# One store of a DMA-bound batched matmul split over two queues, eight engines for a quarter of it

## Chip, cores, metric

The kernel runs on one core of a Trainium2 chip. The metric is the device time of one execution in microseconds (us). All runs quoted here were in the fast state: the granted clock was 0.937 of full speed in the profile before.

## The reference

```python
# x: (32, 512, 1024) float32, weight: (32, 1024, 768) float32
def reference(x, weight):
    return np.matmul(x, weight).astype(np.float32)
```

## The kernel before

For each of 32 batches the kernel loads x (2 MB of float32 in DRAM) and weight (3 MB), converts both to bf16 on the way in (the page counts 1,024 KB for a load of x), transposes x on TensorE, multiplies, and stores 1.5 MB of float32. Every transfer but one is issued from GpSimd to one software queue: in each pass x of batch b+3, then the weights of batch b+3, then the store of batch b−1. Only the store of the last batch goes on SP's queue, in two halves.

```python
AHEAD = 3
...  # cut: pools (w and x 4 buffers, out 7), CHUNKED: weights of the last 4 batches in pieces
out_view = out.rearrange("b (mi mo) n -> b mi (mo n)", mi=P)     # 128 rows of 12,288 B a batch

def load_x(b):
    xs[b] = x_pool.tile([P, MT, K], BF16, name="x_sb")
    nc.gpsimd.dma_start(out=xs[b], in_=x_view[b])
...  # cut: load_w (alike), transpose, matmuls, evacuate

for b in range(B):
    if b + AHEAD < B:
        load_x(b + AHEAD)
        load_w(b + AHEAD)
    if b > 0:
        nc.gpsimd.dma_start(out=out_view[b - 1], in_=outs[b - 1])
    outs[b] = out_pool.tile([P, MT * N], F32, name="out_sb")
    ...  # cut: transposes, matmuls and evacuations of batch b
    # last batch only, after each half:
    #     nc.sync.dma_start(out_view[b, :, cols], outs[b][:, cols])
```

## Time and profile before

| | before |
|---|---|
| time, median of 3 runs | 518.48 us (517.94 to 518.51) |
| software DMA queue, share of 16 engines | 99.9% |
| PE busy | 424.2 us, 82% |
| PE idle for weights | 61.9 us |
| x of the last batch, first and last of 16 landings | 484.26 and 488.88 us |

These are lines of the page of the kernel before: span, busy times, DMA queues (packets, MB, share of 16 engines' span), the summary of the chain that ended last, and the stores as DMA issues (count, KB each, median us from issue to landing).

```profile
span 516.5 us, 5888 instructions
PE 424.2 (82%) x2512; PEld 277.7 (54%) x2560; DVE 127.0 (25%) x192; ACT 76.3 (15%) x129; POOL 53.9 (10%) x106
...
q0 software_dynamic: 14400, 132.65, 99.9%
q1 hardware_dynamic: 288, 1.57, 0.7%
q8 instruction: 20, 0.33, 0.2%
...
DMA 74%; PE 21%; DVE 2%; issue 1%; ACT 0%; POOL 0%; POOLq 0%
...
out_dram<-out_sb POOLq DMA_DIRECT2D x31, 1536.0 KB, 41.9
...
out_dram<-out_sb SPq DMA_DIRECT2D x2, 768.0 KB, 7.0
```

The DMA engines have no idle time: the software queue alone takes 99.9% of them. The 20 packets of q8, which the profile calls an instruction queue, are of 16,384 B and 0.885 to 0.975 us each in the trace; what they carry it does not say. They share engines with the data: each of them sets one engine's data back by about 1.1 us.

The end of the chain of waits (start, duration, what) shows what the last part of the run hangs on.

```profile
457.72 31.16 DMA x_sb<-in_x_dram
488.88 0.04 issue
488.92 0.75 PE pt L67 x4
489.67 1.30 PE pm L85 x8
...
495.00 6.83 PE pm L85 x42
501.88 4.84 PE pm L85 x29
506.74 0.59 ACT out_sb L98
```

PE waits until x of the last batch has landed, at 488.88 us, and has work from there to the end of its own part, near 506.7 us; the last transfer to land is the last store, at 514.61 us. The landing of x is complete only when the last of the 16 engines has delivered its share. Each transfer counts up 16 times, once per engine (the trace has 1,600 packets of 4 B in the software queue for its 100 transfers), so the trace gives the 16 landing times of each. In the kernel before their spread grows from 0.75 us in the first 30 us to 4.62 us for this x. The engines run ahead of or behind each other inside the queue, and PE is fed at the pace of the last.

### The profile page before, as it was taken

How to read it: one execution, taken by the hardware profiler on the slowest of the kernel's cores; microseconds unless marked ns; L12 is line 12 of the kernel's file. 1: busy time of each engine (PE TensorE's matmuls, PEld its weight loads, DVE VectorE, ACT ScalarE, POOL GpSimd, SP SyncE). 2: the span in 40 equal slices, each digit the busy share in tenths (PEclk: the TensorE clock that was granted, in tenths of full speed). 3: DMA queues.
4: the chain of work that ended last, by engine and by line, in shares of the span. 5: the costliest groups of instructions: out<-in, count | busy, mean ns of one | idle time of the engine just before them, and what ended most of it. 6: DMA issues, size and time to landing. Idle time of an engine off the chain costs nothing.

```text
span 516.5 us, 5888 instructions
## 1 busy us (share of the span) xinstructions
PE 424.2 (82%) x2512; PEld 277.7 (54%) x2560; DVE 127.0 (25%) x192; ACT 76.3 (15%) x129; POOL 53.9 (10%) x106
## 2 busy tenths in 40 slices
PE   1799999788887979868897879887887986978992
PEld 1466666455554656545564546554555653655561
DVE  1133333133131331322321213312223121322221
ACT  0011111111111111101110101111111110111111
POOL 3011010100101001100011010010100101111000
PEclk9999999899897998989998979998899897988997
DMA  8999999999999999999999999999999999999996
GB/s 158 217 218 216 211 274 278 272 268 240 263 274 275 278 249 246 279 275 274 266 233 270 278 275 271 245 256 278 273 276 255 245 273 272 276 266 242 256 387 265
DMA packets 14714, 134.60 MB, mean 261 GB/s; under 512 B 1632, under 2 KB 1632, under 8 KB 3040
## 3 DMA queue, kind: packets, MB, share of 16 engines
q0 software_dynamic: 14400, 132.65, 99.9%
q1 hardware_dynamic: 288, 1.57, 0.7%
q8 instruction: 20, 0.33, 0.2%
q14 instruction: 6, 0.05, 0.0%
HBM read 167.77 MB, written 50.33 MB: 422 GB/s over the span
## 4 chain that ended last, share of the span: by engine, by line
DMA 74%; PE 21%; DVE 2%; issue 1%; ACT 0%; POOL 0%; POOLq 0%
DMA w_sb<-in_weight_dram 37%; DMA out_dram<-out_sb 24%; PE pm L85 19%; DMA x_sb<-in_x_dram 13%; PE pt L67 2%; DVE xT L69 1%; DVE out_sb L97 1%; ACT out_sb L98 0%; POOL x_sb L53 0%; POOLq L53 0%; POOLq L59 0%; POOLq L159 0%
## 5 line engine op out<-in xcount | busy, mean ns | idle before, releaser
L85 PE MATMUL pm<-w_sb,xT 128*128 128x256 bf16 (+1 forms) x2000 | 370.7, 340 | 66.6 <-DMA w_sb<-in_weight_dram 61.9
L85 PEld LDWEIGHTS <-xT 128*128 128x128 bf16 x2048 | 207.2, 102 | 204.6 <-issue 72.9
L69 DVE COPY xT<-pt 128x1024 bf16<-128x1024 bf16 x128 | 85.8, 689 | 264.0 <-PE pt L67 264.0
L67 PE MATMUL pt<-ident,x_sb 128*128 128x128 f32 x512 | 80.3, 291 | 15.9 <-DMA x_sb<-in_x_dram 15.6
L67 PEld LDWEIGHTS pt<-ident,x_sb 128*128 128x128 f32 x512 | 76.3, 207 | 24.1 <-issue 14.6
L96 ACT COPY out_sb<-pm 128x512 f32<-128x512 f32 x64 | 37.5, 586 | 287.9 <-PE pm L85 284.5
L97 DVE COPY out_sb<-pm 128x512 f32<-128x512 f32 x64 | 43.9, 687 | 116.2 <-PE pm L85 116.2
L98 ACT COPY out_sb<-pm 128x512 f32<-128x512 f32 x64 | 37.5, 586 | 142.4 <-PE pm L85 142.2
L53 POOL DMA_DIRECT2D x_sb<-in_x_dram x32 | 17.1, 536 | 192.6 <-DMA w_sb<-in_weight_dram 141.8
L59 POOL DMA_DIRECT2D w_sb<-in_weight_dram x37 | 19.7, 532 | 114.2 <-DMA out_dram<-out_sb 56.5
L115 POOL DMA_DIRECT2D out_dram<-out_sb x31 | 16.6, 536 | 136.8 <-DMA x_sb<-in_x_dram 64.7
L96 ACT ACT_TABLE_LOAD x1 | 1.3, 1283 | 0.7 <-PEq L159 0.7
masks.py:199 POOL TENSOR_SCALAR_AFFINE_SELECT ident<-ident 128x128 f32<-128x128 f32 x1 | 0.3, 288 | 0.1
masks.py:197 POOL MEMSET ident<- 128x128 f32 x1 | 0.2, 243 | 0.0
L159 POOL MEMSET const-float32-0.0<- 128x1 f32 x1 | 0.1, 99 | 0.2 <-issue 0.2
L159 POOL MEMSET const-bfloat16-1.0<- 128x1 bf16 x1 | 0.1, 103 | 0.0
L159 POOL MEMSET const-uint8-127<- 128x1 uint8 x1 | 0.1, 103 | 0.0
L159 POOL MEMSET const-float32-1.0<- 128x1 f32 x1 | 0.1, 100 | 0.0
## 6 DMA issues: line engine op xcount, KB each, us to landing
out_dram<-out_sb POOLq DMA_DIRECT2D x31, 1536.0 KB, 41.9
w_sb<-in_weight_dram POOLq DMA_DIRECT2D x28, 1536.0 KB, 43.2
x_sb<-in_x_dram POOLq DMA_DIRECT2D x32, 1024.0 KB, 39.6
w_sb<-in_weight_dram POOLq DMA_DIRECT2D x7, 768.0 KB, 31.4
out_dram<-out_sb SPq DMA_DIRECT2D x2, 768.0 KB, 7.0
w_sb<-in_weight_dram POOLq DMA_DIRECT2D x2, 384.0 KB, 28.7
```

The lines of the kernel that those rows point to most:

```text
L53: nc.gpsimd.dma_start(out=xs[b], in_=x_view[b])
L59: nc.gpsimd.dma_start(out=ws[b][:, at:at + n, :], in_=w_view[b, :, at:at + n, :])
L67: nc.tensor.transpose(pt[:, j, :], pairs[:, mt, j::JT], ident)
L69: nc.vector.tensor_copy(xT.rearrange("p j m r -> p (j m r)"), pt.bitcast(BF16).rearrange("p j m -> p (j m)"))
L85: nc.tensor.matmul(pm[bank][:, at:at + size], xT[:, ko // 2, :, ko % 2], ws[b][:, ko, off:off + size], start=(ko == 0 and not (together an ...
L96: nc.scalar.copy(o[:, 0:512], pm[0])
L97: nc.vector.tensor_copy(o[:, 512:1024], pm[1])
L98: nc.scalar.copy(o[:, 1024:N2], pm[2])
L115: nc.gpsimd.dma_start(out=out_view[b - 1], in_=outs[b - 1])
L159: nc = _bacc.Bacc("TRN2", target_bir_lowering=False, num_devices=1)
```

## The change

The intent is to balance the engines. If some engines are late because they also carry packets of the instruction queue, giving them fewer bytes of one store would let all of them end together. The store of batch 8 is cut: 32 of its 128 rows go as four transfers of eight rows on SP's queue, the other 96 as before.

```diff
+    FEW = {8}
 ...
+    def store(b):
+        first = 0
+        if b in FEW:
+            first = 32
+            for at in range(4):
+                nc.sync.dma_start(out_view[b, at:first:4], outs[b][at:first:4])
+        nc.gpsimd.dma_start(out=out_view[b, first:], in_=outs[b][first:])
 ...
             if b > 0:
-                nc.gpsimd.dma_start(out=out_view[b - 1], in_=outs[b - 1])
+                store(b - 1)
```

The order of instructions on PE, DVE, ACT and GpSimd is unchanged; SP gets four issues.

## The prediction

The sum came to 518.48 - 0.9 = 517.6 us. Terms of it are cut below, because they rested on a rule about the numbers of the engines that no trace here shows: two rows of 0.46 us more, 0.92 us, on each of the eight engines that the 8-row transfers use, and two rows less on each of the other eight. "0-7" and "8-15", here and in the expectations, stand for these two halves and say nothing of the engines' numbers.

> What bounds the kernel. The 16 DMA engines. The page's queue table has the software queue at 99.9% of 16 engines' span, and the chain of waits is 74% DMA, 21% PE. PE is 82% busy and waits 61.9 us for weights. Slack lies only between the engines. The trace's landing records (16 increments per transfer, one per engine) show it: first to last increment is 0.75 us in the first 30 us, 2.4 us at 150 us, 3.5 us at 250 us, 4.6 us from 420 us on. Single engines fall back in steps of about 1.1 us, at the times of the 20 packets of 16,384 B on the instruction queue (about 0.94 us each). The steps go round eight engines in turn (the one hit at 222 us is hit again at 421 us), so about eight engines are never hit, and the four hit at 421 to 496 us end 3.9 to 4.6 us late.[...] The last store lands at 511.1 us on the first engine, at 514.6 us on the last.
>
> What the change does. For batch 8 only, 32 of 128 rows of 12,288 B go as four 8-row transfers.[...] The other 96 rows are 6 per engine.[...] A store row took 0.46 us in the trace[...]. Bytes and the work of PE, DVE, ACT and its order stay; four issues on SP, idle until 506 us, are added.
>
> Critical path. The slowest engine sets the landings of weights and x, and those set PE: x of the last batch lands at 488.9 us, then PE is busy to 506.7 us. If the late engines lie in 8-15, everything after batch 8's store leaves the queue moves 0.9 us earlier; the early engines have about 2 us of slack from 150 us on and do not become the latest. If the late four lie in 0-7, the end is 0.9 us later. This trace gives no engine numbers. That eight engines are hit, and that the amount moved (1.84 us between the halves) fits the spread at that time (2.4 us), makes me believe that the change aims at the right half: three in four.
>
> Prediction: 518.48 - 0.9 = 517.6 us, range 516.7 to 519.4. Chances: faster by over 2% 0.005; within 2% 0.99; slower 0.005.
>
> What would show it. The landing spread after about 190 us falls by about 0.9 us (3.5 to 2.6, 4.6 to 3.7); the hardware queue has about 1.97 MB; x of the last batch lands near 488.0 us; PE busy stays 424 us; the SP stores of batch 8 land within a few us, not 42.
>
> What would make it wrong. The late engines are in 0-7 (then 519.4).[...] PE near its own limit could hide the gain, but it waits on DMA until 489 us.

## The result

The median of six runs is 519.49 us (518.84 to 520.16), against 518.13 us (517.75 to 518.51) for six runs of the kernel before. The ratio of fast runs is 1.0028, 95% interval 1.0015 to 1.0041. A ratio here is the mean time of one kernel's fast runs over that of the other's of the same rounds, so it is not quite the ratio of the medians quoted. The change costs about 1.4 us; the sign is clear, and it is not the predicted one.

The same lines of the page of the changed kernel:

```profile
span 518.1 us, 5899 instructions
PE 425.9 (82%) x2512; PEld 278.1 (54%) x2560; DVE 127.0 (25%) x192; ACT 76.3 (15%) x129; POOL 53.9 (10%) x106
...
q0 software_dynamic: 14368, 132.26, 99.5%
q1 hardware_dynamic: 352, 1.97, 0.9%
q8 instruction: 20, 0.33, 0.2%
...
DMA 88%; PE 9%; issue 1%; DVE 0%; ACT 0%; POOL 0%; POOLq 0%
...
out_dram<-out_sb POOLq DMA_DIRECT2D x30, 1536.0 KB, 42.0
...
out_dram<-out_sb SPq DMA_DIRECT2D x2, 768.0 KB, 5.3
out_dram<-out_sb POOLq DMA_DIRECT2D x1, 1152.0 KB, 41.0
...
out_dram<-out_sb SPq DMA_DIRECT2D x4, 96.0 KB
```

The 0.4 MB moved from q0 to q1 as planned, and nothing else in the totals changed. The chain's share of DMA, 74% before and 88% after, is not evidence of anything: DMA and PE are both mostly busy (99.9% and 82% before), and the chain follows whichever ended last at each step. The control below, which is the kernel before in another spelling, shows 82%.

The end of the chain of the changed kernel:

```profile
459.99 31.17 DMA x_sb<-in_x_dram
491.16 0.04 issue
491.20 0.75 PE pt L68 x4
491.95 1.85 PE pm L86 x8
...
498.92 6.83 PE pm L86 x42
505.80 4.83 PE pm L86 x29
510.65 0.59 ACT out_sb L99
```

The last x landed at 491.16 us, 2.28 us later than before, where the prediction had it near 488.0. From there to the start of the last copy PE took 19.5 us, against 17.9 us before. The windows view (window, its length, busy us and count by engine, clock, DMA share, GB/s) of the last stretch, kernel before and then the changed one:

```profile
488.00:512.00 24.00, 17.68 (x110) 11.38 (x112) 5.47 (x8) 4.64 (x8) 0.53 (x1) 0.94 0.98 365
```

```profile
488.00:512.00 24.00, 19.31 (x110) 12.23 (x112) 5.47 (x8) 4.65 (x8) 0.53 (x1) 0.93 0.92 331
```

The same 110 matmuls took 1.63 us more. In the changed kernel a stretch of 3.4 us at half the clock began at 492.6 us; before, none lay between 478.4 and 509.2 us. This is put down to chance and not to the change: the control below had such a stretch at 488.9 us and still took 517.81 us, and a repeat of the changed kernel had none in this place and took 520.5 us. Nor did it add to the loss: the last store landed at 516.87 us against 514.61 us before, 2.26 us later, which is the delay of the last x and no more.

The landing records are the better witness, because they show all 16 engines. The mean over the 16 landings says how much work the engines had on average; the last says when PE can go on. "Control" is the kernel before rebuilt in the new spelling, with no batch split. Worked out from the landing records, in us, mean and last:

```
transfer           before            control           changed           changed minus control
x of batch 13      200.85 / 202.19   200.77 / 202.35   200.84 / 203.41   +0.07 / +1.06
weights of 13      208.15 / 209.46   208.06 / 209.57   208.71 / 211.75   +0.65 / +2.18
store of 15        306.95 / 309.02   306.96 / 309.22   307.55 / 311.29   +0.59 / +2.07
store of 20        386.15 / 388.02   386.17 / 388.22   386.75 / 390.27   +0.58 / +2.05
x of batch 31      486.25 / 488.88   486.27 / 489.08   486.85 / 491.16   +0.58 / +2.08
```

The x of batch 13 is the first transfer after the split store. By its end the mean is back where it was (+0.07), as it must be if only rows were exchanged, and the last engine is 1.06 us late; at the store of batch 4, before SP's rows, it had been 0.13 us late. Then, within one weight load, the mean itself moves by 0.58 us and the last engine by 1.12 us more, and neither comes back. The second step was not in the prediction at all: no rows were moved there.

Its source can be seen in the packets. A weight row of one engine takes 0.926 us as a packet. Between 203 and 212 us the control has no weight packet over 0.96 us; the changed kernel has 16, the longest 2.29, 2.15 and 1.96 us. Added up, packets in 204 to 212 us are 7.5 us too long. 7.5 us over 16 engines is 0.47 us, most of the 0.58 us. No other cause was found in the trace: PE, DVE, ACT and GpSimd execute the same order, and GpSimd's nearest issue (204.02 to 204.56 us) ends before the first long packet (205.12 us).

The first step is the one that the prediction described, on the wrong engines. The packet records name no engine, but an engine's packets follow each other with fixed gaps (the 0.460 us store rows of one engine start 0.456 to 0.457 us apart at 144.55 to 146.84 us), and the four transfers on SP mark eight of them, so that single engines can be followed through the trace. Lag behind the most advanced engine, in us, of five engines of the changed kernel ("low": carries SP's rows, "high": does not; "q8": start of its 16,384 B packets):

```
engine        at 143 us  at 175 us  at 199 us  at 207 us  at 484 us   q8 at us
low,  late      2.71       4.43       4.11       4.76       6.74      53, 247, 448
low,  late      1.30       3.03       2.70       2.88       4.87      33, 223, 423
high, late      2.01       1.87       2.01       3.10       5.34      74, 273, 475
high, late      1.95       1.81       2.05       3.26       4.18      103, 299
high, first     0.14       0.00       0.01       0.00       0.00      none
```

SP's rows put 1.73 us on both low engines; the 96-row store, with six rows for every engine instead of eight, does not take that back relative to the high ones. So the step is 1.84 us between the halves, as costed (four rows of 0.46 us). But two of the late engines were low ones, and they were the two that had been hit first. After that the two high ones lose 1.1 to 1.2 us between 199 and 207 us, in the long packets.

SP's transfers themselves behaved as predicted. In the timeline of the changed kernel (start, duration, what) SP issues them in three microseconds:

```profile
144.64 3.02 SPq L107 DMA_DIRECT2D out_dram<-out_sb  x4
```

Their landings are at 145 to 156 us. Each has nine increments, one at once (145.81 us for the first) and eight later (150.23 to 151.10 us), and eight packets of 4 B, so eight engines moved data; which eight by number the trace does not show. In the packets SP's rows alternate with packets of the software queue one by one: on one engine an SP row of 0.473 us starts at 148.98 us, then come an x row of 0.624 us, SP's 4 B packet, another x row, and at 150.66 us SP's next row.

### The profile page after: what moved, and what is told of

Same layout as the page of the kernel before. It is cut to its first block, busy times and chain, and to the rows that moved or that the text cites. A ratio compares the mean times of both kernels' runs of the same rounds, so it can differ in the third digit from the quotient of the medians.

```text
span 518.1 us, 5899 instructions
## 1 busy us (share of the span) xinstructions
PE 425.9 (82%) x2512; PEld 278.1 (54%) x2560; DVE 127.0 (25%) x192; ACT 76.3 (15%) x129; POOL 53.9 (10%) x106
## 3 DMA queue, kind: packets, MB, share of 16 engines
q1 hardware_dynamic: 352, 1.97, 0.9%
## 4 chain that ended last, share of the span: by engine, by line
DMA 88%; PE 9%; issue 1%; DVE 0%; ACT 0%; POOL 0%; POOLq 0%
DMA x_sb<-in_x_dram 36%; DMA w_sb<-in_weight_dram 27%; DMA out_dram<-out_sb 25%; PE pm L86 8%; PE pt L68 1%; DVE out_sb L98 0%; DVE xT L70 0%; ACT out_sb L99 0%; POOL x_sb L54 0%; POOLq L108 0%; POOLq L54 0%; POOLq L60 0%; POOLq L169 0%
## 5 line engine op out<-in xcount | busy, mean ns | idle before, releaser
L68 PE MATMUL pt<-ident,x_sb 128*128 128x128 f32 x512 | 80.5, 291 | 18.2 <-DMA x_sb<-in_x_dram 17.9
## 6 DMA issues: line engine op xcount, KB each, us to landing
w_sb<-in_weight_dram POOLq DMA_DIRECT2D x2, 384.0 KB, 28.7
```

The source lines that it names most:

```text
L68: nc.tensor.transpose(pt[:, j, :], pairs[:, mt, j::JT], ident)
```

## The experiments

There were 18 runs, all correct; `again` repeats the changed kernel and `even2` repeats `even`. Each was traced once, and a time of a single traced run is called so. The theories were these:

- Balance: bytes and work are the same, only the unequal rows matter (ten on eight engines, six on the others), and their sign depends on where the late engines are.
- Disturbance: a store that leaves its usual form (in two transfers, or on SP's queue) costs something in itself, even with equal rows.
- Count: more transfers cost more.

Each edit below is relative to the changed kernel. "before" is the median of the kernel before in the same rounds on the same chip.

```
label        edit                                this     before   ratio [95%]
again        none                                519.11   518.17   1.0025 [1.0011, 1.0039]
base         no batch split                      518.31   517.82   1.0006 [0.9993, 1.0018]
even         8: two 16-row on SP + 96            519.61   518.17   1.0034 [1.0019, 1.0048]
even2        same as even                        519.63   517.82   1.0040 [1.0027, 1.0053]
six          8: four 6-row, two 4-row + 96       518.75   518.17   1.0021 [1.0009, 1.0033]
twice        8 and 16: as changed                520.12   518.17   1.0032 [1.0018, 1.0046]
sp128        8: all 128 rows, one on SP          519.80   517.82   1.0036 [1.0024, 1.0049]
pool_split   8: 32 + 96 rows, both GpSimd        519.67   517.82   1.0035 [1.0021, 1.0049]
cols         8: two column halves, GpSimd        518.11   518.07   1.0001 [0.9988, 1.0013]
even_b16     16: as even                         519.06   517.90   1.0029 [1.0012, 1.0046]
eight_b16    16: as changed                      518.80   517.90   1.0018 [1.0006, 1.0031]
four_b16     16: eight 4-row + 96                518.37   517.90   1.0009 [0.9997, 1.0021]
even_b20     20: as even                         518.40   517.90   1.0004 [0.9992, 1.0016]
eight_b20    20: as changed                      518.98   518.08   1.0017 [1.0004, 1.0029]
even_b24     24: as even                         518.37   518.08   1.0008 [0.9995, 1.0022]
eight_b24    24: as changed                      519.19   518.07   1.0016 [1.0002, 1.0029]
four_b24     24: eight 4-row + 96                517.90   518.07   0.9997 [0.9983, 1.0010]
four16_b24   24: four 4-row + 112                517.99   518.08   1.0002 [0.9989, 1.0014]
```

### Repeat and control

`again` is the changed kernel unaltered.

> The change once more, unaltered, to pin its size and to see whether the pattern of late engines is the same in another execution. Theory A (the extra 0.92 us falls on late engines): about +0.9 us against before, and two of the eight engines that carry the 8-row transfers are again the ones that the instruction packets hit first and second in each round of eight. Theory B (the small transfers themselves cost time): also about +0.9 to +1.4, this run does not separate them.

It took 519.11 against 518.17 us, ratio 1.0025: the loss is real. In its trace the two low engines among the hit ones were the third and fourth in the order of hits, not the first two. The mean of the last x was 486.92 us, +0.65 against the control, and again the jump came in the weight load of batch 13 (7.3 us of packet time too much). The last x landed only 0.88 us after the control's, but this run took 520.5 us: the last 16,384 B packet, at 497 us, was again the turn of the fourth in the order, a low one, and the last store of GpSimd's queue ended with a spread of 6.8 us, against 5.3 us before.

`base` asks whether the new spelling alone costs anything. (Besides the line shown, the body of `store` was reduced to the plain store on GpSimd.)

```diff
-    FEW = {8}
+    FEW = set()
```

> The changed file with no batch in the split set, so the program of before. A control: ratio 1.000 within 0.001. Its trace gives a second look at before: if x of the last batch lands at 488.9 us within 0.5 again, the 489.7 us of the even split is an effect; if it lands anywhere between 488.5 and 490, it is not.

It took 518.31 against 517.82 us, ratio 1.0006 with an interval that spans 1. The restructured code costs nothing that can be resolved.

### Equal rows, still split

`even` and `even2` are one kernel, run in two separate sets of rounds. SP gets two transfers of 16 rows, one row for each of 16 engines (the page of `even` has 352 packets on the hardware queue: the 288 of the kernel before, 32 rows, and 16 for each transfer), so that every engine carries eight rows as before: two from SP and six from the rest.

```diff
-            for at in range(4):
-                nc.sync.dma_start(out_view[b, at:first:4], outs[b][at:first:4])
+            for at in range(2):
+                nc.sync.dma_start(out_view[b, at:first:2], outs[b][at:first:2])
```

> The same 32 rows on SP's queue, but as two 16-row transfers, so that all sixteen engines carry 2+6=8 rows as before. Theory A: no engine carries more than before, so the time equals before within 0.3 us. Theory B (the cost is the split, the second queue cutting in, or the 96-row rest): about +1 us, as the change.

> The even split again (two 16-row transfers on SP, 96 rows on the software queue, 8 rows on every engine). Theory A (only unequal rows cost) expects +0.0 to +0.3 us and needs the +1.4 us of the first time to be chance; theory B (the split itself costs) expects +1.0 to +1.5 us again.

Ratios 1.0034 and 1.0040. A pure balance theory needs 1.000 here, and it falls: with equal rows the split costs at least as much as with unequal ones. In the trace of `even2` the mean of the last x was 487.43 us, 1.16 us over the control. The traced run of `even` was its fastest, 518.52 us, and there the mean was only 0.18 us over and the sum of long packets in 204 to 212 us only 1.9 us. So the disturbance varies from run to run, and where it was small the run was near the kernel before: 0.35 us above its median, just above its slowest of 11 runs (518.44 us). That is one run.

`six` makes the transfers smaller, but the shares more unequal. The estimate is that SP's queue puts six rows on each of four engines and four on each of two more, so that with six of the 96 rows these carry twelve and ten, the others six. It takes over from the changed kernel's trace that each row of a small transfer goes to an engine of its own, and the same engines serve each transfer.

```diff
-                nc.sync.dma_start(out_view[b, at:first:4], outs[b][at:first:4])
+                nc.sync.dma_start(out_view[b, at:24:4], outs[b][at:24:4])
+            for at in range(24, 26):
+                nc.sync.dma_start(out_view[b, at:first:2], outs[b][at:first:2])
```

Numbers of engines are cut from theory A's part, and with them the first of its two conditions: that none of the late engines is one to which SP's queue gives rows here. "0 to 5", in the second, stands for the six engines that get them by this estimate.

> The 32 rows as four 6-row transfers and two 4-row transfers. Theory A:[...] no late engine carries more, all late ones lose 0.92 us, and the time is 0.9 us below before (ratio 0.998); if a late engine is among 0 to 5, the time is 0.9 to 1.8 us above. Theory B: about +1 us or a little more, since there are six small transfers in place of four.

Ratio 1.0021: less than `even`, more than nothing. It cannot be told from the changed kernel. Its long packets summed to 3.9 us, its mean of the last x was +0.44, its last landing +1.45, with a spread of 7.17 us.

`twice` does the change at batch 8 and again at batch 16.

```diff
-    FEW = {8}
+    FEW = {8, 16}
```

> The change for batches 8 and 16. Theory A: the late engines of the lower half carry 4 rows more than before, +1.84 us against before. Theory B: twice its cost, also +1.8 to +2.7 us. A rival C (the +1.4 us of the change was chance, or a shift of the PE clock at the end) expects no more than for one batch.

Ratio 1.0032 against 1.0025 of `again` on the same chip: the second split did not add a resolvable second cost, though with intervals this wide its loss, about 1.7 us, does not exclude the 1.84 us that theory A had expected. In its trace the last x landed at 491.83 us, 2.75 us over the control, while the mean was only 0.45 us over: here the spread, not the mean, is what grew.

### Which part of the split disturbs

`sp128` sends the whole store of batch 8 on SP: one transfer, 128 rows, all engines equal (432 packets on the page's hardware queue, 144 more than before: 128 rows and 16 of 4 B).

```diff
-        first = 0
-        if b in FEW:
-            first = 32
-            for at in range(4):
-                nc.sync.dma_start(out_view[b, at:first:4], outs[b][at:first:4])
-        nc.gpsimd.dma_start(out=out_view[b, first:], in_=outs[b][first:])
+        eng = nc.sync if b in FEW else nc.gpsimd
+        eng.dma_start(out=out_view[b], in_=outs[b])
```

> Batch 8's store whole, 128 rows, on SP's queue: no split, no 96-row transfer, but SP's queue cuts in ahead of the loads that wait. If the cutting in costs (theory B1): +1 us or more. If the 96-row transfer[...] costs (B2): 0.0 within 0.3 us. Theory A: 0.0 within 0.3 us.

`pool_split` keeps SP out of it: 32 and 96 rows, both on GpSimd's queue.

```diff
-            for at in range(4):
-                nc.sync.dma_start(out_view[b, at:first:4], outs[b][at:first:4])
+            nc.gpsimd.dma_start(out=out_view[b, :first], in_=outs[b][:first])
```

> Batch 8's store as 32 and 96 rows, both on the software queue, 2+6 rows on each engine. B2 (the 96-row transfer costs): +1 us. B1 (SP's queue cutting in costs): 0.0 within 0.3 us. Theory A: 0.0 within 0.3 us.

`cols` splits by columns instead: two transfers on GpSimd, each of all 128 rows and 6,144 B of each row.

```diff
-        first = 0
         if b in FEW:
-            first = 32
-            for at in range(4):
-                nc.sync.dma_start(out_view[b, at:first:4], outs[b][at:first:4])
-        nc.gpsimd.dma_start(out=out_view[b, first:], in_=outs[b][first:])
+            for cols in (slice(0, N2), slice(N2, 2 * N2)):
+                nc.gpsimd.dma_start(out=out_view[b, :, cols], in_=outs[b][:, cols])
+            return
+        nc.gpsimd.dma_start(out=out_view[b], in_=outs[b])
```

> Batch 8's store as two halves of its columns, each 128 rows of 6,144 B, both on the software queue: one transfer more, as in pool_split, but[...] no queue cuts in. If a transfer that shifts rows between engines sets off the long load packets: 0.0 within 0.4 us and no group of long packets at 204 to 208 us. If any change in the sequence of transfers does: +1.4 to +1.9 us, as pool_split.

`sp128` took 519.80 against 517.82 us (1.0036) and `pool_split` 519.67 against 517.82 us (1.0035), so neither SP's queue nor unequal rows is needed. `cols` took 518.11 against 518.07 us (1.0001): two transfers instead of one cost nothing. The count theory falls. The profile of `pool_split` and then of `cols`, as DMA issues of the split store and as the landing that the end hangs on:

```profile
out_dram<-out_sb POOLq DMA_DIRECT2D x1, 1152.0 KB, 35.3
out_dram<-out_sb POOLq DMA_DIRECT2D x1, 384.0 KB, 39.2
...
460.01 31.17 DMA x_sb<-in_x_dram
491.17 0.04 issue
```

```profile
out_dram<-out_sb POOLq DMA_DIRECT2D x2, 768.0 KB, 37.5
...
458.38 31.15 DMA x_sb<-in_x_dram
489.54 0.04 issue
```

Both have two transfers with the same total bytes in the same place of the same queue. One ends its last x at 491.17 us, the other at 489.54. The landing records show the jump in the first and not in the second (mean landing minus the control's, us; the sum of the lengthening of packets in 204 to 212 us):

```
             x of 13   weights of 13   x of 31   long packets, 204-212 us
changed       +0.07        +0.65        +0.58         7.5
again         +0.10        +0.58        +0.65         7.3
even2         +0.79        +1.18        +1.16         6.0
pool_split    +0.28        +0.92        +0.95         9.6
sp128         +0.71        +0.76        +0.68         0.3; 6.8 at 148-180 us
even          +0.16        +0.30        +0.18         1.9
cols          +0.17        +0.18        +0.11         none
before        +0.08        +0.09        -0.02         none
```

What the weights of batch 13 show stays to within about 0.1 us. `even2` had an earlier group of long packets, about 7 us at 158 to 162 us, some 8 us after SP's rows had landed (150.4 us), and `sp128` had nearly all of its at 163 to 166 and 177 to 179 us, after its store on SP had landed (157.9 us).

Is the lengthening the split's, or would it have come anyway? The window of 204 to 212 us can be read in all 20 traces. The seven with 96 rows of batch 8 on GpSimd (changed, `again`, `even`, `even2`, `six`, `twice`, `pool_split`) have 1.9 to 9.6 us of it. Of the twelve in which that store is not split, or split as in `cols`, eleven have none and one, `eight_b16`, has 1.7 us. (The twentieth is `sp128`.) So the split brings it, but long packets also come without a split: 2.9 us at 214 to 216 us in `eight_b24`, and 3 to 9 us at 60 to 72 us in every trace. The 1.9 us of `even` is no more than that, and a mean within about 0.3 us of the control's is not a sign of a split either (`even_b24` stood at +0.31 at the x of batch 13, long before its own).

The last landings of the two queues' kernels that matter agree: for `sp128` the chain shows

```profile
459.93 31.18 DMA x_sb<-in_x_dram
491.11 0.04 issue
...
508.97 0.59 ACT out_sb L99
```

and from there to the last copy PE took 17.9 us at full clock, as before the change.

What sets `cols` apart from `pool_split`? In `cols` every row stays in a transfer of 128 rows; in `pool_split` the 128 rows are dealt out anew, two and six to an engine by an estimate (32 and 96 rows over the 16 engines; six is also what the 1.84 us between the halves of the changed kernel fits). It is natural to say that rows moved to other engines than their usual ones. That is an argument and not a measurement: the records name no engine, and `sp128`, which keeps one transfer of 128 rows, disturbs as well (1.0036), from SP's queue. What happens inside the engines to make the packets long, and why 5 to 10 us later in a load, is not settled.

### The same at other batches

If the cost were the unequal rows alone, it would not fade when the split is done later, and equal rows would be free at every batch.

`even_b16`, `even_b20` and `even_b24` are `even` with

```diff
-    FEW = {8}
+    FEW = {16}    # {20}, {24}
```

`eight_b16`, `eight_b20` and `eight_b24` are the change itself with that line alone.

> The even split (two 16-row transfers on SP, 96 rows on the software queue), at batch 16 in place of 8. In the traces of every split at batch 8 load packets grow long at 204 to 208 us, about 10 us after the 96-row store lands, while the second split of the run twice left no such trace. Theory B (any split of any store costs about 1.5 us): +1.0 to +1.8 us, with a group of long load packets near 334 us. Theory D (the disturbance belongs to batch 8's place in the program): 0.0 within 0.4 us and no such group.

> The change itself at batch 16. Theory A plus D: the two instruction-hit engines among 0 to 7 gain 0.92 us; when they are two of the four latest, +0.9 us, else -0.5 to 0; so a wide spread of single runs round +0.5 us. Theory B: +1.4 to +2 us.

> The even split at batch 20. Theory B: +1.0 to +1.8 us. Theory D: 0.0 within 0.4 us. If it differs from batch 16's, the place in the program decides.

> The change at batch 20, beside even_b20's +0.2 us. If unequal rows cost: +0.6 to +1.2 us, and in the trace the engine last at x of the last batch is one that carried the 8-row transfers. If not: +0.2 us within 0.4.

> The even split (two 16-row transfers on SP) at batch 24, beside eight_b24's +0.8 us. If the unequal rows carry that: even_b24 0.0 to +0.3 us, single runs within 0.5 us of one another, x of the last batch within 0.4 us of 489.0. If the split carries it: +0.6 us or more.

> The change at batch 24, where the even split's disturbance should be small. The unequal rows alone: each execution has two instruction-hit engines among 0 to 7; where these are two of the four hit last, +0.9 us and x of the last batch near 489.9 us, else about -0.5 us. So +0.3 us in the middle and a spread of 1 us or more between single runs. If the unequal rows cost nothing and only the disturbance counts: 0.0 to 0.2 us, single runs as close as before's.

With equal rows the cost is 1.0029 at batch 16, 1.0004 at 20 and 1.0008 at 24; with eight-row transfers 1.0018, 1.0017 and 1.0016. The mean landing, followed through each of these traces, grows less by the split than at batch 8, where it grew by about 0.6 us in the two traces of the change. Difference to the control before the split and after it, us:

```
             before the split    after it            growth
even_b16     s12  +0.06          s17  +0.25          0.19
eight_b16    s12  +0.32          s17  +0.44          0.12
even_b20     s16  -0.09          s21  +0.03          0.12
eight_b20    s16  -0.13          s21  +0.16          0.29
even_b24     s20  +0.21          s25  +0.44          0.23
eight_b24    s20  +0.21          s25  +0.49          0.28
```

(s12 is the store of batch 12, and so on.) So by the mean the disturbance is smaller there, in every one of the six traces. It is not harmless: in `even_b24` three long packets at 415 to 417 us (1.81, 1.64 and 1.11 us) fell on the two latest engines, and the last x landed at 490.32 us, 1.24 us after the control's, with a mean of only +0.44 and equal rows. That traced run, its slowest, took 519.75 us, where an x within 0.4 us of 489.0 had been expected. What counts is where the long packets fall, and not only their sum.

For batch 16 the smaller growth does not settle the time: the traced run of `even_b16` was its fastest, 518.08 us, and its slow runs were not traced. At 20 and 24 one might hope to tell rows and disturbance apart: the unequal kernel is 0.0013 and 0.0008 dearer than the equal one, or 0.4 to 0.7 us. That fits rows on late low engines (0.92 us if the latest engine is one of them), but the intervals overlap, and in the traces the order is mixed: the last x is 0.06 us before the control's in `even_b20` and 0.96 us after it in `eight_b20`, but 1.24 us after it in `even_b24` and 0.53 us in `eight_b24`. In `eight_b20` the last engine to deliver the last x was one that carried SP's rows. The price of unequal rows by themselves is not resolved.

### Aiming at fewer engines

The prediction's idea was to relieve the late engines. The remaining kernels try it with four-row transfers, which four engines carry in the traces, so that late engines elsewhere are relieved.

`four_b16` and `four_b24`: 32 rows as eight transfers of four rows.

```diff
-    FEW = {8}
+    FEW = {16}    # {24}
 ...
-            for at in range(4):
-                nc.sync.dma_start(out_view[b, at:first:4], outs[b][at:first:4])
+            for at in range(8):
+                nc.sync.dma_start(out_view[b, at:first:8], outs[b][at:first:8])
```

`four16_b24`: 16 rows as four transfers of four, and 112 rows (seven per engine) on GpSimd.

```diff
-    FEW = {8}
+    FEW = {24}
 ...
-            first = 32
+            first = 16
```

Engines without SP's rows lose two rows (0.92 us) of the 32, or one (0.46 us) of the 16.

> Batch 16, the 32 rows as eight 4-row transfers[...]. Theory A plus D:[...] -0.5 to -0.9 us, x of the last batch lands at 488.0 to 488.4 us. Theory B: +1 us or more, x at 490 us or later.

> Eight 4-row transfers at batch 24[...]. In the trace of four_b16 none of the instruction-hit engines carried the 4-row transfers. So all late engines lose 0.92 us: -0.6 to -0.9 us, x of the last batch at 488.0 to 488.4 us, first landing 483.4. If only the disturbance counts: 0.0 to +0.3 us, x at 488.9 or later.

> Batch 24, 16 rows as four 4-row transfers, 112 rows on the software queue, 7 on each engine[...]. So the late engines lose 0.46 us[...]. Unequal rows alone: -0.3 to -0.5 us, x of the last batch near 488.5 us. With a disturbance like even_b24's on top: 0.0 within 0.4 us.

Ratios 1.0009, 0.9997 and 1.0002. In the traces of `four_b16` and `four_b24` none of the four engines that carry SP's rows was hit by a 16,384 B packet, so the twelve others, all late ones among them, lost 0.92 us of work. In `four_b24` the relief can be read off the landings. The last engine, minus the control's, us:

```
weights of 25   +0.38      store of 24   -0.64      x of 30   -0.57      x of 31   -0.01
```

From the split on, the last landing is 1.02 us earlier than it had been, the 0.92 us of the rows and a tenth. This is the predicted mechanism with its predicted size, on engines that were the right ones in this execution. Between the x of batches 30 and 31 it is lost: an engine with SP's rows and three small packets (8,192 B on q14, 0.3 to 0.5 us each) became the last, at 489.07 us. In `four_b16` nothing is gained at all: its last x landed at 489.34 us, 0.25 us after the control's, where 488.0 to 488.4 had been expected. `four16_b24`, with half the amount, ended its last x at 488.88 us and took 517.78 us in that run, inside the scatter of the kernel before. No version beat the kernel before by more than the noise.

## Why the prediction was wrong

1. DMA bounds the kernel and its slowest engine sets the time: right. In nearly every traced run the total was the last landing of the last x plus 28.7 to 29.7 us (29.4 before, 29.0 changed; 30.5 in one run of `again`).
2. The steps of 1.1 us come with the 16,384 B packets and go round eight engines: right. In the followed traces a hit sets its engine back about 1.1 us (1.07 to 1.33 in the control), with a period of eight. In the trace before the packets' own times show the same period: 0.893, 0.892, 0.951, 0.944, 0.936, 0.966, 0.974 and 0.961 us, and then 0.893, 0.893, 0.949 us and so on. In the control an engine hit three times ended 4.05 to 4.78 us behind, the engines not hit at most 1.7 us (4.50 to 4.61 and 2.25 us in the kernel before). For a kernel at 99.9% of its DMA engines the cost is not hidden, and by the end it is a spread of 4.6 us.
3. Eight-row transfers use eight engines, 96 rows are six per engine, 0.46 us a row, so 0.92 us either way: right. Each of the four had eight late increments, and the halves parted by 1.73 to 1.84 us.
4. "makes me believe that the change aims at the right half: three in four": this is the step that failed. Six of the eight hit engines do lie in the high half, the one without SP's rows, but two do not. Which two in the order of hits differs from execution to execution: first and second, third and fourth, or fifth and sixth in the traces followed. In five of six such traces those two were among the four that are hit three times. In the changed kernel's trace they were the two hit first, and the change put 0.92 us on the latest engine of all. The spread grew from 4.62 to 6.80 us, where the prediction had 3.7. Before the run nothing showed engine numbers; counting eight hit engines and eight engines in a half was taken for evidence that they are the same eight.
5. "Bytes and the work of PE, DVE, ACT and its order stay", and therefore only the balance matters: the term that was missing. The split lengthened packets of a later weight load by 7.5 us in sum, moved the mean of all 16 engines by 0.58 us for the rest of the run, and single late engines by about 1.1 us. `even`, `even2`, `pool_split` and `sp128`, with equal rows, cost 1.0034 to 1.0040, as much as or more than the change. So a split without unequal rows is enough for the whole loss of 1.4 us.
6. "If the late four lie in 0-7, the end is 0.9 us later", 519.4: that came within 0.1 us of the result, but partly for the wrong reason. In the changed trace 1.06 us of the last landing's 2.08 us stood before the long packets and agree with it; 1.02 us are the rest. How the median's 1.4 us divides between rows and disturbance was not resolved: the traced run was the second longest of its six (520.12 us).
7. PE busy near 424 us and hardware queue 1.97 MB: right, 425.9 us and 1.97 MB; the 1.7 us of PE is the half-clock stretch. SP's stores landing in a few us: right, all within 11 us and not 42.

Open: what the 16,384 B packets carry, which numbers the engines have, what makes the packets long, why they come 5 to 10 us after the store, why they also come in some places without a split, why splits at batches 20 and 24 do it less, and the price in time of the unequal rows alone.

## What to carry to other kernels

In a queue that is full, compare the mean of the 16 landings with the last: if the mean moves, work was added; if only the last moves, balance was lost (at the x of batch 13 here +0.07 us in the mean and +1.06 us in the last; one load later +0.65 and +2.18 us). Before moving bytes between engines, find out which engines are late, and whether they are the same ones in each execution; here they were not, so a fixed shift from one half to the other cannot be relied on. And test the vehicle apart from the cargo: an edit that splits the transfer but keeps the shares equal would have shown the cost of the split before any theory of balance.
